# Three of four later modulations summed over rows of w_ada, and queries scaled before they are turned, in a fused trunk layer

## The chip, the core and the metric

The kernel runs on one core of one Trainium2 chip. The metric is the time of one execution on the device in microseconds, the median of several runs. The core's engines are named as the profile names them: PE is TensorE's matmul, PEld its weight load, DVE is VectorE, ACT is ScalarE, POOL is GpSimd, SP is SyncE, which issues nearly all the DMAs.

## What is computed

The program is one layer of a transformer trunk, for 128 context tokens and 512 latent tokens, 1024 wide, all in float32. Two things of it matter here: the modulation, six rows of 1024 for each of the two conditioning vectors, and the attention with its normalised queries.

```python
sh1, sc1, g1, sh2, sc2, g2 = jnp.split(silu(c) @ w_ada + b_ada, 6, axis=-1)   # for c and for c_ctx
u = rms_norm(h, p["g_pre1"]) * (1 + sc1) + sh1
mo, k, v = mixer(u, p, rope_tabs, ctx_k, ctx_v)
h = h + g1 * rms_norm(mo, p["g_post1"])
u = rms_norm(h, p["g_pre2"]) * (1 + sc2) + sh2
h = h + g2 * rms_norm(conv_ffn(u, p), p["g_post2"])
# in mixer:
q, k = rms_norm(q, p["q_norm"]), rms_norm(k, p["k_norm"])      # a head at a time
q_used, keys, vals = rope(q), concat(ctx_k, rope(k)), concat(ctx_v, v)   # latent tokens
att  = softmax(q_used @ keys.T * HEAD_DIM ** -0.5) @ vals @ p["w_att_out"]
conv = (b_gate * dwconv3(c_gate * x_in, p["conv_w"])) @ p["w_conv_out"]
return (sigmoid(g_att) * att + sigmoid(g_conv) * conv) @ p["w_o"], k, v
```

`sh1` and `sc1` are needed at the start. The other four rows, `g1`, `sc2`, `sh2` and `g2`, are needed only after the mixer; these are the later modulations.

## The kernel before

Each product of float32 matrices is made from three products on TensorE: both operands are cut into a high part in a reduced format (fp32r) and the rest (`mm3`, L156). ScalarE copies the high part (`whi`), VectorE subtracts it (`wlo`). Weights come in units of 512 KB into `raw_tile()`, a ring of three buffers; `fetch`, `cut_upto` and `next_unit` load and cut a unit ahead.

The order on TensorE, ScalarE, VectorE and, in the prologue, SP is written out by hand: each engine takes its instructions in the order in which the program states them, and waits where an operand or a buffer is not there yet. The order on SP and POOL is the scheduler's elsewhere.

The stages, with the borders that the profile shows:

- Prologue (to about 75 us): the first modulation, keys and values.
- Attention (75 to 283 us): four groups `g` of four query heads. A group has steps `i` = 0 to 8. `Step(g)` (i = 0) scores the context queries (`scores`, L589), and steps 1 to 8 score one latent tile of 128 queries for two heads each. `most` (L727, L729) takes the row maxima, `exps` (L742) the exponentials with their sums, `shares` (L748, L752) divides on POOL, `turned` (L760, L765) transposes the probabilities, and VectorE or ScalarE copies them out of PSUM as `PT` (L770), `values` (L780, L789) multiplies with the values.
- The queries of tile `t` of group `g`, called (g, t), tile 0 being the context: `q_part` makes them in PSUM, `q_rotate` (`rotate`, L513 to L525) multiplies by the gains and turns the pairs into `qf`; the final sum for latent tiles is L525 on POOL. `squares` and `factors` (L527 to L537) make `rq`, one factor per token and head: ScalarE squares, VectorE sums (L535), POOL scales (L536) and takes the power -0.5 (L537). `q_turn` (L557 to L568, transposes in L560) transposes `qf`, ScalarE and VectorE cut it into `QH` and `QL`. The factor itself is applied behind the scores: `most` multiplies the maxima by `rq`, `exps` has `rq` as its scale.
- In step i, `first` and `then` name the tile that is turned: (g, 2) in step 0, (g, 3) in step 2, (g, 4) and (g+1, 0) in step 5, (g+1, 1) in step 7. The tile (g+1, 2) is made in step 7 of group g and gets its factors in `after2` of step 8; (0, 3) is made ahead of the loop, and `third` gives its rotation and factors in step 1 of group 0, with the turning in step 2.
- Between these, `ada_use` computes the later modulations: 32 units of `w_ada` (1024 rows by 128 columns) in 16 blocks of two. `ada_mm` (L205 to L210) multiplies a unit, as the moving operand, by a 32-column piece of `s32` that holds the two vectors silu(c) and silu(c_ctx) at a place that shifts from unit to unit; each of the four quarters of the array's columns takes two of the eight k-tiles. So 16 units land in different rows of one PSUM tile, and `ada2_keep` adds it to `acc`. `CUTS` and `ring` state in which order units of `w_ada` and of the other weights use the ring of raw buffers. After the loop `ada2_fold` adds the four quarters with `sel`, adds the bias, and multiplies by the gains into `mod`, columns by feature.
- `w_att_out` (283 to 340 us): `plain_gemm`, eight output tiles j of two blocks. While j < 6, twelve pieces of `making` form the combined right-hand sides (`T1` to `T4`) of the next stage. After j = 0 `mod_rows` transposes `mod`, and one DMA writes the 64 rows of the four modulations to `bct` in DRAM.
- The pairs (340 to 574 us): 19 steps m of `mix`, seven block products each, a fast (Strassen) form for the gates and the convolution's inputs. `AH`, `AL` (regions r2 and r3) are free from here, and are taken by `BH`, `BL`.
- `w_conv_out` (574 to 630 us): `plain_gemm` over `BH`, `BL`.
- `w_o`, first half: four quarters q of `us` (630 to 657 us), each quarter all five token tiles, L157 to L159; beside them the weights of the second half are loaded and cut (`half_load`, `half_cut`, L1661 to L1668), and `bload` (L1355 to L1358) spreads the rows `g1` from `bct` over 128 partitions into `WR`. `half_cut(3)` stands in the first quarter. `ZB0`, `ZB1`, `ZB2` (regions r0, r1, r2) hold the right-hand sides of the feed-forward stage.
- Second half of `w_o` with the residual and the second norm (`modulated` is the first to use `sc2` and `sh2`), then the feed-forward network to the end at 1134 us, where `finish` uses `g2`.

The region r0/r1 holds `UH`, `UL` (the normalised input) until the pairs end.

## Time and profile before

| | us |
|---|---|
| median of 3 runs | 1135.46 (1135.44 to 1135.54) |
| span of the profiled execution | 1134.1 |
| PE busy in the attention, 75.0 to 283.5 | 205.04 of 208.50 |
| PE busy in `w_att_out`, the pairs and `w_conv_out`, 283.5 to 629.9 | all 346.4 |
| POOL busy in the attention | 118.89 of 208.50 |
| PE busy behind the first half of `w_o`, 657.5 to 1134.0 | 467.61 of 476.50 |

The page gives the busy time of each engine; the stages are cut out by time windows, whose columns are the busy microseconds and the number of instructions of PE, PEld, DVE, ACT and POOL, the granted TensorE clock, the share of the DMA engines and GB/s. A timeline row has the start and the busy time of an instruction (or of a run of like ones, with "x" their number), engine, line, operation, output and input, shapes, and in brackets how long the engine had stood idle before it, and what released it.

### The profile page before, as it was taken

To read this page: it belongs to the slowest core of one execution; us is meant where nothing else is said; L and a number is where in the kernel's file an instruction comes from. 1 tells how busy PE (TensorE), PEld (TensorE's weight loads), DVE (VectorE), ACT (ScalarE), POOL (GpSimd) and SP (SyncE) were. 2 spreads that over 40 slices of the span, in tenths; PEclk is the share of its full clock that TensorE was granted. 3 is DMA by queue.
4 is the path that set the end of the run, shared out by engine and by line. 5 is a ranking of instruction groups with operands and counts; after the bars stand their busy time and mean duration, and the time that the engine had idled before them with its cause. 6 is when DMAs were issued, how large, how long until landed. Compare 5 with 4: busy or idle time off the path is not lost.

```text
span 1134.1 us, 19512 instructions
## 1 busy us (share of the span) xinstructions
PE 1114.9 (98%) x7885; PEld 1024.5 (90%) x7885; DVE 796.3 (70%) x1269; ACT 569.9 (50%) x979; POOL 158.9 (14%) x198
## 2 busy tenths in 40 slices
PE   7999999999999999999999999999999999999997
PEld 6787888888999999999999889999999999998786
DVE  4587666654656798889645458888788778888544
ACT  4375666665234444545522256655554545555431
POOL 2056566652000000000000012000000000002001
PEclk9999999999999999999999999999999999999999
DMA  9632433333222223223332644233333323315732
GB/s 335 205 92 82 126 94 112 110 96 112 76 75 75 75 77 105 81 75 95 93 111 76 207 164 150 76 99 99 98 112 109 95 91 109 105 61 186 240 99 93
DMA packets 177304, 129.58 MB, mean 114 GB/s; under 512 B 6274, under 2 KB 159422, under 8 KB 177214
## 3 DMA queue, kind: packets, MB, share of 16 engines
q1 hardware_dynamic: 177102, 128.30, 36.4%
q8 instruction: 62, 1.02, 0.4%
q14 instruction: 28, 0.23, 0.1%
q10 hardware_dynamic: 112, 0.04, 0.0%
HBM read 116.87 MB, written 11.45 MB: 113 GB/s over the span
## 4 chain that ended last, share of the span: by engine, by line
PE 89%; DVE 3%; ACT 1%; POOL 0%; issue 0%; DVEq 0%; POOLq 0%; ACTq 0%
PE b L1030 45%; PE b L159 9%; PE b L157 9%; PE b L158 9%; PE s L789 3%; PE s L765 3%; PE s L589 3%; PE s L157 2%; PE s L159 2%; PE s L158 2%; PE s L209 1%; DVE Y L1514 1%; DVE wlo L693 0%; PE s L560 0%; PE b L1421 0%; DVE mx L727 0%
## 5 line engine op out<-in xcount | busy, mean ns | idle before, releaser
L1030 PE MATMUL b<-ZB,whi 128*128 128x322 f32 x1024 | 228.6, 310 | 0.0
L1030 PEld LDWEIGHTS b<-ZB,whi 128*128 128x128 f32 x1024 | 173.8, 189 | 1.6
L1030 PE MATMUL b<-ZB,wlo 128*128 128x322 f32 x512 | 159.4, 311 | 0.0
L1030 PE MATMUL b<-MT,whi 128*128 128x320 f32 x608 | 134.1, 308 | 0.0
L1030 PEld LDWEIGHTS b<-MT,whi 128*128 128x128 f32 x608 | 101.7, 188 | 0.0
L1030 PEld LDWEIGHTS b<-ZB,wlo 128*128 128x128 f32 x512 | 96.2, 188 | 0.0
L1030 PE MATMUL b<-MT,wlo 128*128 128x320 f32 x304 | 93.8, 308 | 0.0
L752 POOL TENSOR_TENSOR pr<-pr,sm 128x640 f32<-128x640 f32 x64 | 80.7, 1270 | 61.1 <-DVE sm L751 61.1
L1017 ACT ACTIVATE whi<-SUM 128x1024 fp32r<-128x1024 f32 x40 | 42.2, 1055 | 79.6 <-DVE SUM L1484 77.2
L1514 DVE SCALAR_TENSOR_TENSOR Y<-C,cffn,Y 128x642 f32<-128x642 f32 x88 | 80.8, 920 | 0.9
L742 ACT ACTIVATE pr<-s,mx,rq 128x640 f32<-128x640 f32 x64 | 56.7, 886 | 38.5 <-DVE mx L729 36.4
L132 DVE TENSOR_TENSOR wlo<-raw,whi 128x1024 fp32r<-128x1024 f32 (+1 forms) x32 | 34.9, 1090 | 52.3 <-ACT whi L131 51.8
L1030 PE MATMUL b<-UH,whi 128*128 128x320 f32 x228 | 70.5, 309 | 0.0
L1030 PE MATMUL b<-UL,whi 128*128 128x320 f32 x228 | 70.4, 309 | 0.0
L1030 PE MATMUL b<-UH,wlo 128*128 128x320 f32 x228 | 70.2, 308 | 0.0
L1021 DVE TENSOR_TENSOR wlo<-raw,whi 128x1024 fp32r<-128x1024 f32 (+1 forms) x51 | 50.4, 1019 | 25.2 <-ACT whi L1017 24.3
L1017 ACT ACTIVATE whi<-WB 128x1024 fp32r<-128x1024 f32 x38 | 40.1, 1056 | 54.8 <-DVE WB L1125 54.8
L157 PE MATMUL s<-whi,UH 128*128 128x256 f32 (+1 forms) x200 | 65.8, 329 | 0.5 <-ACT UH L376 0.4
L727 DVE TENSOR_REDUCE mx<-s 128x1 f32<-128x640 f32 x64 | 52.5, 820 | 17.5 <-PE s L589 17.2
L158 PE MATMUL s<-wlo,UH 128*128 128x256 f32 (+1 forms) x200 | 61.5, 308 | 2.2 <-DVE wlo L693 2.2
L1038 ACT ACTIVATE p<-b 128x322 f32<-128x322 f32 (+1 forms) x78 | 34.3, 439 | 58.2 <-PE b L1030 58.2
L159 PE MATMUL s<-whi,UL 128*128 128x256 f32 (+1 forms) x200 | 61.8, 309 | 0.3
(322 smaller groups left out, 2933.0 us busy)
## 6 DMA issues: line engine op xcount, KB each, us to landing
raw<-in_w_in_dram SPq DMA_DIRECT2D x48, 512.0 KB, 3.6
RAW<-in_w_up_dram SPq DMA_DIRECT2D x40, 512.0 KB, 3.8
raw<-in_w_ada_dram SPq DMA_DIRECT2D x32, 512.0 KB, 4.0
raw<-in_w_down_dram SPq DMA_DIRECT2D x22, 512.0 KB, 4.2
actd<-Y SPq DMA_DIRECT2D x18, 321.0 KB, 2.5
AFB<-actd SPq DMA_DIRECT2D x18, 321.0 KB, 6.8
XT<-in_w_ada_dram SPq DMA_DIRECT2D x9, 512.0 KB, 8.5
raw<-in_w_conv_out_dram SPq DMA_DIRECT2D x9, 512.0 KB, 4.1
```

The source lines that it names most:

```text
L132: eng.tensor_tensor(out=lo[:, :n], in0=raw, in1=hi[:, :n].bitcast(F32), op=ALU.subtract)
L157: PE.matmul(out, ah, bh, start=start, stop=False)
L158: PE.matmul(out, ah, bl, start=False, stop=False)
L159: PE.matmul(out, al, bh, start=False, stop=stop)
L727: V.tensor_reduce(out=mx, in_=self.sc[h], axis=AX.X, op=ALU.max, negate=True)
L742: S.activation(pr, self.sc[h], AF.Exp, bias=mx, scale=rs, accum_out=sm)
L752: G.tensor_tensor(out=pr, in0=pr, in1=sm.broadcast_to((128, NTOK)), op=ALU.mult)
L1017: S.activation(to[0], raw, AF.Copy)
L1021: V.tensor_tensor(out=lo, in0=raw, in1=hi.bitcast(F32), op=ALU.subtract)
L1030: PE.matmul(out, p[:, ws], q[:, k, :], start=start and k == 0 and n == 0, stop=stop and k == 3 and n == 2, skip_group_check=True)
L1038: S.activation(t, pair[j][b], AF.Copy)
L1514: V.scalar_tensor_tensor(out=y, in0=crows(j)[i][:, d:d + NACT], scalar=cffn[:, 44 * d + o:44 * d + o + 1], in1=y, op0=ALU.mult, op1=ALU.add)
```

## The change

It has two parts.

The queries: `q_even` takes the place of `factors` for the tiles made in the loop and for (0, 3). Behind the factors it multiplies `qf` by `rq` on POOL, and notes the tile in the set `even`. For these tiles `most` and `exps` no longer multiply by `rq`; their scale is 1. The turning (`q_turn`, `q_turn_both`) now reads the scaled query. Tiles (0, 0), (0, 1), (0, 2) keep the old way.

The modulations: only `g2` is still made by `ada_use`, in four blocks: one ahead of the loop, and one at step 6 of groups 0 to 2. `ring` is shortened to match. For the other three, the product silu(c) @ w_ada is taken by rows: a DMA loads 128 rows by 1024 columns of `w_ada` (`row_load_ada`), each partition's row is multiplied by its own scalar for the two vectors and added up over the eight row blocks, so that two sums of [128, 1024] are left, and `row_fold` sums over the partitions with a matrix of ones (32 columns) on TensorE, 4 quarters of 256 columns for each vector.

- `g1` during `w_att_out`: `gate_term` at the places `GATE_AT` (VectorE; the first term on ScalarE), rows in `GR`, which has r6b until `T4` takes it at j = 7; the sums lie in `MS`. The pieces of `making` move to `MAKE_AT`. `row_fold`, bias, gain and the DMA to `bct` stand at j = 7 ahead of the preparation for the pairs.
- `sc2` during the pairs m = 0 to 5: `scale_term` multiplies on ScalarE (16 terms, in slots of `mix`); all but the first of each vector go into one of four places of `SP`, from which a DMA issued by POOL with `accum_op=add` adds them to the sum in `SC`. At m = 6 `mod_rows_of` folds, copies and writes the rows to `srow`; `BH`, `BL` take r2, r3 only then.
- `sh2` during `w_conv_out`: `shift_term(j - 1)` at the head of step j on VectorE (first on ScalarE), the rows in `SR` (r1), the sums in `SA` (r0); the last term stands in the first quarter of `w_o`, the fold in front of the second. `room_for` gives r0 and r1 to the feed-forward right-hand sides only behind that.
- `srow` is read back as `srows`, and one transpose with `finished`, behind the first tile of `w_o`'s second half, puts `sc2` and `sh2` into `mod`.

```diff
-        ada_load(ada_raw[i], (2, 4, 3, 5)[i // KT] * D + (i % KT) * 128)
+        ada_load(ada_raw[i], 5 * D + i * 128)
...
         for n in range(2):
-            ada_mm(p, ada_raw[2 * i + n], 2 * ((2 * i + n) % 16), n == 0, n == 1)
+            ada_mm(p, ada_raw[2 * i + n], 2 * (2 * i + n), n == 0, n == 1)
...
     def ada2_keep(i, p, acc):
-        a = acc[:, i // KT * 128:i // KT * 128 + 128]
-        if i % KT == 0:
-            V.tensor_copy(a, p)
+        if i == 0:
+            V.tensor_copy(acc, p)
         else:
-            V.tensor_tensor(out=a, in0=a, in1=p, op=ALU.add)
+            V.tensor_tensor(out=acc, in0=acc, in1=p, op=ALU.add)
+
+    def finished(which, src):
+        b = F_B + (2, 4, 3, 5)[which] * KT
...
     def ada2_fold(acc):
         p = ps1()
-        for i in range(2):
-            PE.matmul(p[:, 32 * i:32 * i + 32], acc[:, i * 128:(i + 1) * 128], sel, start=True, stop=True)
...
+        PE.matmul(p[:, 0:32], acc, sel, start=True, stop=True)
+        finished(3, p[:, 0:16].rearrange("p (f r) -> p r f", r=2))
+
+    def row_term(accs, raw, k):
+        for v in range(2):
+            s = s32[:, 32 * k + 30 + v:32 * k + 31 + v]
+            if k == 0:
+                S.activation(accs[v], raw, AF.Copy, scale=s)
+            else:
+                V.scalar_tensor_tensor(out=accs[v], in0=raw, scalar=s, in1=accs[v], op0=ALU.mult, op1=ALU.add)
+
+    def row_fold(p, accs):
+        for v in range(2):
+            for j in range(4):
+                PE.matmul(p[32 * j:32 * j + 32, 256 * v:256 * v + 256], ones, accs[v][:, 256 * j:256 * j + 256], start=True, stop=True,
+                          tile_position=(0, 32 * j))
+
+    def quarters(x):
+        return x.rearrange("v (j c) -> j v c", c=256)
+
+    def row_load_ada(dst, which, k):
+        nc.sync.dma_start(dst, w_ada[k * 128:(k + 1) * 128, which * D:(which + 1) * D])
...
+        even = set()
+
+        def q_even(sq, g, t):
+            factors(sq, rq[g][:, t, :])
+            G.tensor_tensor(out=qfs[g, t], in0=qfs[g, t], in1=rq[g][:, t, :].unsqueeze(2).broadcast_to((128, 4, HD)), op=ALU.mult)
+            even.add((g, t))
...
-        acc = both[1].rearrange("p a d -> p (a d)")[:, 0:256]
+        acc = both[1].rearrange("p a d -> p (a d)")[:, 0:128]
...
-        ring = ada_raws(0, 1) + [("u", 10), ("u", 11)] + ada_raws(1, 4) + [("u", 12)] + ada_raws(4, 5) + [("u", 13)] + ada_raws(5, 8)
-        ring += [("u", 14)] + ada_raws(8, 9) + [("u", 15)] + ada_raws(9, 12) + [("u", 16)] + ada_raws(12, 15) + [("u", 17)]
-        ring += ada_raws(15, 16) + [("u", 18)]
+        ring = ada_raws(0, 1) + [("u", 10), ("u", 11)] + ada_raws(1, 2) + [("u", 12), ("u", 13)] + ada_raws(2, 3)
+        ring += [("u", 14), ("u", 15)] + ada_raws(3, 4) + [("u", 16), ("u", 17), ("u", 18)]
...
-                    V.tensor_tensor(out=self.mx, in0=self.mx, in1=rq[self.g][:, 0, :], op=ALU.mult)
+                    self.rs = [1.0] * 4
+                    if (self.g, 0) not in even:
+                        V.tensor_tensor(out=self.mx, in0=self.mx, in1=rq[self.g][:, 0, :], op=ALU.mult)
+                        self.rs = [rq[self.g][:, 0, i:i + 1] for i in range(4)]
...
-                rs = rq[self.g][:, 1 + 2 * qh + qi, 2 * pi + h:2 * pi + h + 1]
-                V.tensor_tensor(out=mx, in0=mx, in1=rs, op=ALU.mult)
+                t, rs = 1 + 2 * qh + qi, 1.0
+                if (self.g, t) not in even:
+                    rs = rq[self.g][:, t, 2 * pi + h:2 * pi + h + 1]
+                    V.tensor_tensor(out=mx, in0=mx, in1=rs, op=ALU.mult)
...
-                                     scale=rq[self.g][:, 0, i:i + 1], accum_out=self.sm[:, i:i + 1])
+                                     scale=self.rs[i], accum_out=self.sm[:, i:i + 1])
...
-            after2.append(lambda: factors(sq, rq[0][:, 3, :]))
+            after2.append(lambda: q_even(sq, 0, 3))
...
-                if i in (4, 6, 8) or (i == 1 and g):
+                if i == 6 and g < 3:
                     ada_use(n_ada)()
...
-                        after2.append(lambda: factors(sq, rq[qt[0]][:, qt[1], :]))
+                        after2.append(lambda: q_even(sq, *qt))
...
+    ones = sm_.tile([128, 32], F32, name="ones", bufs=1)
+    G.memset(ones, 1.0)
...
-    for name, tag in (("T1", "r5a"), ("T2", "r5b"), ("T3", "r6a"), ("T4", "r6b")):
+    def turned_sum(name, tag):
         z = rb.tile([128, 2, 4, HT], F32R, tag=tag, name=f"M{name}")
...
+    for name, tag in (("T1", "r5a"), ("T2", "r5b"), ("T3", "r6a")):
+        turned_sum(name, tag)
+    GR = rb.tile([128, 2, D], F32, tag="r6b", name="GR")
+    GACC = [MS[:, v * D:(v + 1) * D] for v in range(2)]
+    row_load_ada(GR[:, 0, :], 2, 0)
+    row_load_ada(GR[:, 1, :], 2, 1)
+
+    def gate_term(k):
+        row_term(GACC, GR[:, k % 2, :], k)
+        if k + 2 < KT:
+            row_load_ada(GR[:, k % 2, :], 2, k + 2)
...
-    Xa, Xb, Xc, Xd = quad(WA, 0), quad(WA, 1), quad(WB, 0), quad(WB, 1)
+    Xa, Xb, Xc, Xd = quad(WA, 0), quad(WA, 1), quad(WB, 0), quad(WA, 0)
...
+    MAKE_AT = (0, 0, 1, 1, 2, 2, 3, 3, 4, 5, 6, 7)
+    GATE_AT = (1, 1, 2, 3, 4, 5, 5, 6)
...
+        if j == 7:
+            turned_sum("T4", "r6b")
+        for i, f in enumerate(making):
+            if MAKE_AT[i] == j:
                 f()
-        elif j == 7:
+        for k in range(KT):
+            if GATE_AT[k] == j:
+                gate_term(k)
+        if j == 5:
+            nc.sync.dma_start(WA[0:128:32, 1280:1536], b_ada[2 * D:3 * D].rearrange("(j c) -> j c", c=256))
+            nc.sync.dma_start(WA[0:128:32, 1536:1792], g_post1[0].rearrange("(j c) -> j c", c=256))
+        if j == 7:
+            pg = bank(3)
+            row_fold(pg, GACC)
+            grow = WA[:, 1792:2304].rearrange("p (v c) -> p v c", v=2)
+            bias, gain = (WA[:, c:c + 256].unsqueeze(1).broadcast_to((128, 2, 256)) for c in (1280, 1536))
+            V.tensor_tensor(out=grow, in0=pg.rearrange("p (v c) -> p v c", v=2), in1=bias, op=ALU.add)
+            V.scalar_tensor_tensor(out=grow, in0=grow, scalar=D ** 0.5, in1=gain, op0=ALU.mult, op1=ALU.mult)
+            nc.sync.dma_start(quarters(bct[0:2 * KT, :].rearrange("(v f) c -> v (f c)", v=2)), grow[0:128:32])
             adds = msums(0)
             adds[0]()
             mhi(0, 0)
@@ -1235,11 +1297,36 @@
...
-            mod_rows(0, 4, sm_, bank(7))
-
...
-    BH = region(ra, "r2", [KT, NTOK], F32R, "BH")
-    BL = region(ra, "r3", [KT, NTOK], F32R, "BL")
+            mod_rows(3, 1, sm_, bank(7))
+
+
+    SC = region(ra, "r2", [5, D], F32, "SC")
+    SP = region(ra, "r3", [5, D], F32, "SP")
+    sums_of, scaled_rows = [SC[:, 0, :], SC[:, 1, :]], [0]
+    row_load_ada(SC[:, 2, :], 4, 0)
+    row_load_ada(SC[:, 3, :], 4, 1)
+    row_load_ada(SC[:, 4, :], 4, 2)
+
+    def scale_term():
+        k, v = divmod(scaled_rows[0], 2)
+        scaled_rows[0] += 1
+        if k >= KT:
+            return
+        room, to = SC[:, 2 + k % 3, :], sums_of[v]
+        if k:
+            to = SP[:, (2 * k + v) % 4, :]
+        S.activation(to, room, AF.Copy, scale=s32[:, 32 * k + 30 + v:32 * k + 31 + v])
+        if k:
+            G.dma_start(out=sums_of[v], in_=to, accum_op=ALU.add)
+        if v and k + 3 < KT:
+            row_load_ada(room, 4, k + 3)
+
+    def mod_rows_of(n, p, accs, to):
+        row_fold(p, accs)
+        S.activation(to, p, AF.Copy)
+        nc.sync.dma_start(quarters(srow[2 * n:2 * n + 2, :]), to[0:128:32, :].rearrange("p (v c) -> p v c", v=2))
+
+    BHL = []
...
+        if m == 6:
+            mod_rows_of(0, bank(5), sums_of, SP[:, 4, 0:512])
+            BHL += [region(ra, f"r{2 + i}", [KT, NTOK], F32R, f"B{x}") for i, x in enumerate("HL")]
+        elif m < 6:
+            for slot in ((0, 3, 4) if m else (1, 3, 4)):
+                also(slot, scale_term)
...
+    SR = region(ra, "r1", [5, D], F32, "SR")
+    SA = region(ra, "r0", [5, D], F32, "SA")
+
+    def shift_term(k):
+        row_term([SA[:, v, :] for v in range(2)], SR[:, k % 5, :], k)
+        if k + 5 < KT:
+            row_load_ada(SR[:, k % 5, :], 3, k + 5)
+
+    for k in range(5):
+        row_load_ada(SR[:, k, :], 3, k)
...
+        if j:
+            shift_term(j - 1)
         _, hi, lo = cut["v", j]
-        outs = plain_gemm(j + 2, hi, lo, BH, BL)
+        outs = plain_gemm(j + 2, hi, lo, *BHL)
...
-    ZB0 = ra.tile([128, 4, 4, HALF], F32R, tag="r0", name="ZB0")
-    ZB1 = ra.tile([128, 4, 4, HALF], F32R, tag="r1", name="ZB1")
-    ZB2 = ra.tile([128, 4, 4, HALF], F32R, tag="r2", name="ZB2")
-    for i, (z, a) in {"B11": (ZB0, 0), "B21": (ZB0, 2), "B22": (ZB1, 0), "T2": (ZB1, 2), "T1": (ZB2, 0), "T3": (ZB2, 2)}.items():
-        TT[i] = (z[:, a], z[:, a + 1])
+    def room_for(tag, one, two):
+        z = ra.tile([128, 4, 4, HALF], F32R, tag=tag, name=f"ZB{tag}")
+        for i, name in enumerate((one, two)):
+            TT[name] = (z[:, 2 * i], z[:, 2 * i + 1])
+
+    room_for("r2", "T1", "T3")
...
+            room_for("r1", "B22", "T2")
...
+        if q == 0:
+            shift_term(KT - 1)
+        elif q == 1:
+            mod_rows_of(1, bank(5), [SA[:, v, :] for v in range(2)], SA[:, 4, 0:512])
+            srows = sm_.tile([64, 128], F32, tag="mrow", name=nm("srows"), bufs=1)[0:32, :]
+            nc.sync.dma_start(srows, srow.rearrange("r (f c) -> (r f) c", c=128))
+            room_for("r0", "B11", "B21")
...
+    pf = bank(7)
+    PE.transpose(pf[:, 0:32], srows, ident[0:32, 0:32])
+    for n in range(2):
+        finished(1 + n, pf[:, 16 * n:16 * n + 16].rearrange("p (r f) -> p r f", r=2))
```

More of the change, by code (lines that the diff above doesn't have):

```diff
@@ L188, in trunk_layer @@
     bct = dp.tile([64, 128], F32, name="bct")
+    srow = dp.tile([4, D], F32, name="srow")
     hd = dp.tile([NT, 128, D], F32, name="hd")
@@ L232, in ada2_fold @@
+    def finished(which, src):
+        b = F_B + (2, 4, 3, 5)[which] * KT
+        V.tensor_tensor(out=mod[:, which], in0=src, in1=feat[:, b:b + KT].unsqueeze(1).broadcast_to((128, 2, KT)), op=ALU.add)
+        if which != 2:
+            gn = (F_POST1, F_PRE2, None, F_POST2)[which]
+            V.tensor_tensor(out=mod[:, which], in0=mod[:, which], in1=feat[:, gn:gn + KT].unsqueeze(1).broadcast_to((128, 2, KT)),
+                            op=ALU.mult)
     def ada2_fold(acc):
         p = ps1()
-        for i in range(2):
-            PE.matmul(p[:, 32 * i:32 * i + 32], acc[:, i * 128:(i + 1) * 128], sel, start=True, stop=True)
@@ L236, in ada2_fold @@
-        for which in range(4):
-            src = p[:, 16 * which:16 * which + 16].rearrange("p (f r) -> p r f", r=2)
-            b = F_B + (2, 4, 3, 5)[which] * KT
-            V.tensor_tensor(out=mod[:, which], in0=src, in1=feat[:, b:b + KT].unsqueeze(1).broadcast_to((128, 2, KT)), op=ALU.add)
-            if which != 2:
-                gn = (F_POST1, F_PRE2, None, F_POST2)[which]
-                V.tensor_tensor(out=mod[:, which], in0=mod[:, which], in1=feat[:, gn:gn + KT].unsqueeze(1).broadcast_to((128, 2, KT)),
-                                op=ALU.mult)
+        PE.matmul(p[:, 0:32], acc, sel, start=True, stop=True)
@@ L966, in trunk_layer @@
                 last = st
-        assert 2 * n_ada == 4 * KT and at_ring[0] == len(ring)
+        assert 2 * n_ada == KT and at_ring[0] == len(ring)
         state["limit"], state["next"] = 1 << 20, 18
```

6 lines of the change are left out of this document (2 added, 4 removed).

## The prediction

> **What bounds the kernel now.** I read the page's busy times first, then the chain that ended last.
>
> ```profile
> span 1134.1 us, 19512 instructions
> PE 1114.9 (98%) x7885; PEld 1024.5 (90%) x7885; DVE 796.3 (70%) x1269; ACT 569.9 (50%) x979; POOL 158.9 (14%) x198
> PE 89%; DVE 3%; ACT 1%; POOL 0%; issue 0%; DVEq 0%; POOLq 0%; ACTq 0%
> ```
>
> TensorE is busy for 98% of the span and makes 89% of the chain. A TensorE instruction taken out is worth its distance in the queue, and a wait put into that queue costs its whole length, unless a later wait shrinks by as much. So I list what leaves the queue, what enters it, and each new wait.
>
> **What leaves.** A block `ada_use` is 16 small products in 32 instructions. One near 172 us, with its neighbours:
>
> ```profile
> 168.18 2.38 PE L789 MATMUL s<-PT,VV 128*64 128x256 f32 x20
> 170.49 1.31 PE L765 MATMUL s<-ident,pr 128*128 128x128 f32 x10
> 171.73 1.08 PE L209 MATMUL s<-raw,s 128*32 128x128 f32 x32
> 172.74 0.33 PE L589 MATMUL s<-KCH,QH 64*128 64x128 f32 x2
> 173.56 0.44 PE L560 MATMUL s<-ident,qf 128*128 128x128 f32 x2
> ```
>
> From the block's start to the next start is 172.74 - 171.73 = 1.01 us. Twelve of sixteen blocks go: -12.1 us.
>
> **What enters.** Three folds (`row_fold`), each 8 products of 256 columns on 32 rows of the array, 16 instructions if they split as the block's do. The nearest row is L789: 20 instructions of 256 columns, on two halves of the array, in 170.49 - 168.18 = 2.31 us, 0.116 each. On four quarters half of that: 16 x 0.058 = 0.92 us a fold, +2.8 us (bounds: the block's 1.01 below, L789's undivided 0.116, so 1.85, above: 2.8 to 5.6, and I stay with the quarters because the blocks run so). One transpose of 32 columns more: +0.2.
>
> **Queries scaled before they are turned.** This is where I expect the gain to be lost. Before, the turning transposes (L560) need only the rotated query; the factors `rq` come later and are used by the softmax. After, POOL multiplies the query by `rq` first, and TensorE waits for it in order, with all that stands behind it. For tile (g+1, 2) the factors are made at the end of step 8 of a group, and the transposes come in step 0 of the next, right behind its 12 score products. The rows of that place:
>
> ```profile
> 172.42 0.41 DVE L535 TENSOR_REDUCE ssq<-sq 128x4 f32<-128x256 f32 x1
> 173.08 1.52 DVE L693 TENSOR_TENSOR wlo<-raw,whi 128x1024 fp32r<-128x1024 f32 x1
> 162.52 0.19 POOL L536 TENSOR_SCALAR ssq<-ssq 128x4 f32<-128x4 f32 x1
> 168.31 0.73 POOL L525 TENSOR_TENSOR qf<-qf,zt 128x256 f32<-128x256 f32 x1 [0.62 <-DVE qf L524]
> 172.27 1.25 POOL L752 TENSOR_TENSOR pr<-pr,sm 128x640 f32<-128x640 f32 x1 [0.34 <-DVE sm L751]
> 173.60 1.05 POOL L536 TENSOR_SCALAR ssq<-ssq 128x4 f32<-128x4 f32 x1
> 174.74 1.02 POOL L537 TENSOR_TENSOR rq<-ssq,mhalf 128x4 f32<-128x4 f32 x1
> ```
>
> POOL finishes the softmax of step 8, then the sum's scaling, then the power: 174.74 + 1.02 = 175.76. The new product has L525's size, 0.73: 176.49. TensorE, with its block gone, is at the transposes at 173.56 - 1.01 = 172.55. It waits 3.9 us, at three transitions (g = 0, 1, 2): +11.8. The POOL times do not come earlier with the shorter queue: they hang on step 8's own transposes, which stand where they stood within the step. L536 took 1.05 instead of 0.19 beside VectorE's subtraction; without that the wait is 3.1, the lower bound 9.2; above, 12.5 if the product meets another such subtraction for 0.2.
>
> [...]
>
> The other tiles have a step between, as (2, 3) here:
>
> ```profile
> 184.34 1.02 POOL L537 TENSOR_TENSOR rq<-ssq,mhalf 128x4 f32<-128x4 f32 x1
> 188.17 0.38 PE L560 MATMUL s<-ident,qf 128*128 128x128 f32 x2
> ```
>
> POOL's power ends at 185.36, the product at 186.1, and the transposes stand at 187.2 with the block gone; so they cost nothing, with about 1 us to spare. But tile (0, 3) has no step between:
>
> ```profile
> 85.93 0.38 PE L560 MATMUL s<-ident,qf 128*128 128x128 f32 x2
> 86.59 3.45 POOL L752 TENSOR_TENSOR pr<-pr,sm 128x640 f32<-128x640 f32 x2
> 87.11 3.47 DVE L693 TENSOR_TENSOR wlo<-raw,whi 128x1024 fp32r<-128x1024 f32 x2
> 88.97 0.39 PE L158 MATMUL s<-wlo,UH 128*128 128x256 f32 x1 [1.09 <-DVE wlo L693]
> 93.10 0.39 PE L158 MATMUL s<-wlo,UH 128*128 128x256 f32 x1 [1.16 <-DVE wlo L693]
> ```
>
> As built, POOL's product stands behind both products L752 of this step: 86.59 + 2 x 1.25 + 0.73 = 89.8, against 85.93, a wait of 3.9. VectorE waits too (its `QL` needs the transposes, the subtractions stand behind it), so the wait at 88.97 stays, but the subtractions no longer collide with POOL, and the wait of 1.16 mostly goes: +2.6 (0 to 4).
>
> **Waits that the blocks covered.** After step 4 of each group, and step 6 of the last, the next scores follow one block sooner. They need the PSUM tile that VectorE still empties:
>
> ```profile
> 198.80 0.82 DVE L770 COPY PT<-s 128x640 f32<-128x640 f32 x1 [0.84 <-PE s L765]
> 199.24 1.08 PE L209 MATMUL s<-raw,s 128*32 128x128 f32 x32
> ```
>
> The copy ends at 199.62, the scores could start at 199.24: 0.38 us, five times, +1.9 (0 to 2). The products `mx` by `rq` that fall away on VectorE lie beside TensorE's work and are worth nothing here, nor are the adds of `acc`.
>
> **The three stages that sum rows.**
>
> ```profile
> 283.50:340.20 56.70, 56.70 (x389) 56.66 (x388) 32.23 (x30) 19.10 (x26) 0.00 (x0) 1.00 0.26 75
> 340.20:573.60 233.40, 233.40 (x1594) 233.40 (x1593) 182.74 (x266) 114.58 (x178) 0.00 (x0) 1.00 0.29 83
> 573.60:629.90 56.30, 56.30 (x386) 56.30 (x385) 28.00 (x37) 14.45 (x18) 0.18 (x3) 1.00 0.32 96
> 665.39 1.28 DVE L1404 SCALAR_TENSOR_TENSOR WR<-TX,root,WR 128x1024 f32<-128x1024 f32 x1 [0.31 <-POOL root L1396]
> 666.59 0.68 DVE L1388 TENSOR_TENSOR TX<-b,WR 128x512 f32<-128x512 f32 x1
> 642.64 1.06 ACT L1017 ACTIVATE whi<-raw 128x1024 fp32r<-128x1024 f32 x1 [7.60 <-DMA raw<-in_w_o_dram]
> ```
>
> Columns are PE, PEld, DVE, ACT, POOL, clock, DMA, GB/s. A term of a row costs VectorE 666.59 - 665.39 = 1.20 us (same form and size), ScalarE 1.06. First stage: 14 x 1.20 = 16.8 on VectorE's 32.2 of 56.7: it fits. Placed by j, VectorE is through with the last term at about 332.4, and TensorE's fold (one eighth before the stage's end) is due at 332.4: +0.3 (0 to 2). The loads `GR` go on SP one step ahead, and the weights behind them two steps ahead: nothing. Second: 16 terms on ScalarE in six pairs of 233.4/19 = 12.3 us, 17 of 74 us, where half is free. The first term waits for its row, issued when `AH` is last read; ScalarE then has 5 us behind it and needs them: +0.3 (0 to 2). Third: 28.0 + 16.8 of 56.3: fits.
>
> The third fold does not. It stands ahead of the second quarter of `w_o`, and the last shift term stands behind the subtraction of the weights for `half_cut(3)` on VectorE. SP, as built, now issues that load behind the two of `bct` into `WR`, which wait for the last product of the stage before:
>
> ```profile
> 627.39 0.37 SPq L1663 DMA_DIRECT2D raw<-in_w_o_dram  x1
> 629.91 0.82 SPq L1357 DMA_DIRECT2D WR<-bct  x2
> 634.32 1.22 DVE L1021 TENSOR_TENSOR ZB<-raw,ZB 128x1024 fp32r<-128x1024 f32 x1
> 636.76 0.39 PE L157 MATMUL b<-whi,MHa 128*128 128x512 f32 x1
> 629.90:636.70 6.80, 6.80 (x31) 5.58 (x31) 5.64 (x6) 3.58 (x4) 0.17 (x3) 1.00 0.90 306
> L139 SPq DMA_DIRECT2D raw<-in_w_o_dram x4: 368/368/395, 606.3 to 634.4; - x4
> DMA to landing us min/median/max: 6.3/6.3/6.3
> ```
>
> So the load goes out at 630.7 instead of 627.4, behind 1 MB more, at 306 GB/s in all: 1.5 MB take 5 us, and it lands at 635.7 (a neighbour took 6.3). ScalarE 1.06, subtraction 1.22, two terms 2.4, half a fold 0.5: 640.9, where 636.6 + 0.9 = 637.5 was due: +3.4. Bounds: 0, if SP's order costs nothing; 5.4 with a landing of 7.
>
> **The accumulating DMAs.** Fourteen, seven in a chain for each row, issued on POOL, which is idle there. No row shows one. Below, a plain load; above, three passes, 10.8:
>
> ```profile
> raw<-in_w_in_dram SPq DMA_DIRECT2D x48, 512.0 KB, 3.6
> ```
>
> The first goes out some 9 us into the pairs, the fold stands at 6 x 12.3 = 73.9: each may take 65/7 = 9.3 us before anything waits, ScalarE's ring of four rooms included. I take about 6, with no wait. [...]
>
> **Sum.** -12.1 + 2.8 + 0.2 + 11.8 + 2.6 + 1.9 + 0.3 + 0.3 + 3.4 = +11.2, so a span of 1145.3. The runs' median, 1135.46, lies 1.4 above the profiled span; I keep that: 1146.7 us. Adding the lower bounds gives -12.1 + 2.8 + 0.2 + 9.2 = +0.1, the upper -12.1 + 5.6 + 0.2 + 12.5 + 4 + 2 + 2 + 2 + 5.4 = +21.6; they won't all fall on one side, so this case's own range is 1139 to 1153.
>
> **Rivals.**
> - *The TensorE sum alone* (11%): no new wait. For it speaks that TensorE is the bound; against it that POOL would have to end each product at 172.6, not 176.5: it decides only if the chain ahead of the product is 3.9 us shorter. -12.1 + 3.0 = -9.1: 1126.4 us.
> - *The transitions alone* (9%): only the three waits at their lower bound cost, the rest finds cover in TensorE's queue: +0.1, 1135.6 us. The 1 us to spare elsewhere speaks for it; SP's order against it.
> - *The accumulations are the bound* (14%): at 10.8 us each the chain of seven ends at 9 + 75.6 = 84.6, 10.7 us past its fold, so ScalarE and then TensorE stand: 1157.4 us. It decides from 9.3 us on. A plain load's 3.6 speaks against it.
> - *The change does not do what it says*: as built, 192 of the small products are gone and 14 accumulations there, so no chance is kept for this.
>
> **Numbers.** The forecast has 66%, 1146.7. The range, 1136 to 1155, holds nearly all of it and what lies toward the two middle rivals. About 0.2%, 2.3 us, is what a measurement can tell from no change. Faster: the first rival and a part of the second, 0.13. Same: the rest of the second, 0.07. Slower: 0.80.
>
> **What would show it.** Right: TensorE's waits in front of the turning transposes, released by POOL, of near 4 us three times in step 0 and one near 85 us; blocks L209 down to four; a wait of some 3 us in front of the third fold, released by VectorE; POOL's DMAs under 9.3 us each. Wrong: transposes that start within 1 us of the scores' end; no wait at the third fold; a fold at the seventh pair that waits for a DMA.

## The result and the profile after

The changed kernel takes 1160.18 us (median of 4 runs, 1158.49 to 1164.11) beside 1135.45 (1134.21 to 1135.54): ratio 1.0226, 95% interval 1.0207 to 1.0245. The direction was forecast; of the 24.7 us, 11.2 were. The profiled execution has a span of 1157.8 us, 23.7 more than before. From its page and from the view of TensorE's waits (who waited for whom, microseconds in total, times, longest):

```profile
span 1157.8 us, 18950 instructions
PE 1119.2 (97%) x7548; PEld 1025.6 (89%) x7548; DVE 819.1 (71%) x1226; ACT 583.6 (50%) x1001; POOL 179.9 (16%) x230
```

```profile
PE s L587 <- POOL qf L581: 15.2, 4, 3.9
PE b L256 <- DVE SA L251: 4.1, 1, 4.1
PE b L1063 <- DVE WB L1074: 2.7, 1, 2.7
PE b L157 <- ACT ACTa L1635: 2.0, 1, 2.0
```

The three upper waits are new. L587 is the turning, L256 the fold, L1063 a block product of the pairs; the fourth is as in the kernel before. TensorE has 337 instructions less, and yet more busy time, 1119.2 us instead of 1114.9. That is the first sign of what the prediction left out: the instructions that remain got slower.

Where the time goes, by stage, worked out from the starts of the first product of each stage in the two timelines (attention: from the first context scores of group 0; the last border but one is the first product with the weights that `half_cut(3)` makes):

| stage | before | after | forecast difference | measured |
|---|---|---|---|---|
| attention | 209.88 | 219.42 | +4.2 | +9.5 |
| `w_att_out` | 56.43 | 57.63 | +1.2 | +1.2 |
| pairs | 234.07 | 240.31 | +1.2 | +6.2 |
| `w_conv_out` | 56.32 | 56.31 | 0 | 0 |
| `w_o` to the weights of `half_cut(3)` | 30.83 | 38.74 | +4.3 | +7.9 |
| rest | 473.40 | 472.38 | +0.2 | -1.0 |

The transition from group 1 to group 2, on POOL and on TensorE, as the prediction worked it out from the same place before:

```profile
177.31 1.25 POOL L783 TENSOR_TENSOR pr<-pr,sm 128x640 f32<-128x640 f32 x1 [0.65 <-DVE sm L782]
178.64 1.05 POOL L556 TENSOR_SCALAR ssq<-ssq 128x4 f32<-128x4 f32 x1
179.78 1.02 POOL L557 TENSOR_TENSOR rq<-ssq,mhalf 128x4 f32<-128x4 f32 x1
180.87 0.61 POOL L581 TENSOR_TENSOR qf<-qf,rq 128x256 f32<-128x256 f32 x1
```

```profile
176.77 0.33 PE L616 MATMUL s<-KCH,QH 64*128 64x128 f32 x2
...
181.54 0.67 PE L587 MATMUL s<-ident,qf 128*128 128x128 f32 x2 [3.88 <-POOL qf L581]
```

The chain on POOL is the forecast one (1.05 and 1.02 again, the product 0.61 instead of 0.73), and the wait of 3.88 us the forecast 3.9. What comes next was not forecast. Windows of TensorE at that place; columns are the window, its length, PE busy and its number, the granted clock, the DMA share, GB/s:

```profile
172.00:177.60 5.60, 5.60 (x56) 1.00 0.01 1
177.60:181.60 4.00, 0.12 (x3) 1.00 0.15 38
181.60:185.00 3.40, 3.40 (x17) 0.50 0.36 109
185.00:190.00 5.00, 5.00 (x47) 1.00 0.01 3
```

After the wait TensorE is granted half its clock for 3.4 us; the two transposes of L587 take 0.67 us where they took 0.44. In windows of 0.1 us, all such stretches between the first scores and the end of the FFN:

| behind the wait at | wait, us | half clock from - to | length | busy time lost |
|---|---|---|---|---|
| tile (0, 3) | 3.57 | 89.4 - 92.9 | 3.41 | 1.7 |
| (1, 2) | 3.88 | 127.0 - 133.8 | 6.83 | 2.7 |
| (2, 2) | 3.88 | 181.6 - 185.0 | 3.41 | 1.7 |
| (3, 2) | 3.88 | 232.8 - 239.6 | 6.83 | 2.9 |
| pairs | 2.69 | 389.8 - 393.2 | 3.41 | 1.7 |
| third fold | 4.13 | 656.1 - 662.9 | 6.83 | 2.5 |

Lost is taken as half of the time in which TensorE was busy at half clock, 13.2 us in all, an estimate: behind the third fold, products of 512 columns started 0.43 us apart at half clock (661.10 to 662.80) and 0.23 us apart after it. The kernel before has one stretch in these stages, 1052.7 to 1056.1 in the feed-forward network (1.7 us); the changed one has none there, and its rest is 1.0 us shorter.

In all six of the table the granted clock is 0.50; three last 3.41 us and three 6.83 us.

The wait in the pairs has another cause. SP's load, VectorE and TensorE there:

```profile
375.77 0.38 SPq L1155 DMA_DIRECT2D raw<-in_w_in_dram  x1
```

```profile
386.55 0.69 DVE L1170 TENSOR_TENSOR WB<-raw 128x512 f32<-128x512 f32 x1 [4.05 <-DMA raw<-in_w_in_dram]
```

```profile
388.39 0.53 PE L1063 MATMUL b<-MT,whi 128*128 128x320 f32 x2 [2.69 <-DVE WB L1074]
```

A load of weights that went out at 375.77 landed at 386.5, 10.7 us later, where the median was 3.9 in this stage before. The next two fences have the stage's windows (PE, PEld, DVE, ACT, POOL, clock, DMA share, GB/s), before and after; the last line is from the view of the DMAs (median to landing):

```profile
350.00:410.00 60.00, 60.00 (x411) 60.00 (x410) 46.55 (x67) 30.67 (x48) 0.00 (x0) 1.00 0.31 88
```

```profile
360.00:420.00 60.00, 57.31 (x379) 56.84 (x378) 42.32 (x58) 39.95 (x56) 12.09 (x14) 0.97 0.99 227
```

```profile
SC<-SP POOLq DMA_DIRECT2D x14, 512.0 KB, 6.4
```

An accumulating DMA takes 6.4 us, close to the 6 assumed, and the fold of this row never waits for it. But the DMA engines, 31% busy here before, are at 99%.

The third fold waits along the chain that the prediction worked out. SP, ScalarE, VectorE, TensorE:

```profile
646.73 0.81 SPq L1463 DMA_DIRECT2D WR<-bct  x2
647.64 0.38 SPq L1769 DMA_DIRECT2D raw<-in_w_o_dram  x1
```

```profile
654.30 1.06 ACT L1050 ACTIVATE ZBr<-raw 128x1024 fp32r<-128x1024 f32 x1 [4.35 <-DMA raw<-in_w_o_dram]
```

```profile
656.54 2.47 DVE L251 SCALAR_TENSOR_TENSOR SA<-SR,s,SA 128x1024 f32<-128x1024 f32 x2
```

```profile
657.87 2.28 PE L256 MATMUL b<-SA,ones 128*32 128x256 f32 x16 [4.13 <-DVE SA L251]
```

The load stands behind the two of `bct`, lands 6.7 us after its issue, and the last shift term comes behind its subtraction. The fold itself takes 2.28 us here, where one at full clock took 1.07: its second half waits for the second vector's term, at half clock.

### The profile page after: what moved, and what is told of

Read it like the earlier page. It is cut to its first block, busy times and chain, and to the rows that moved or that the text cites. A ratio compares the mean times of both kernels' runs of the same rounds, so it can differ in the third digit from the quotient of the medians.

```text
span 1157.8 us, 18950 instructions
## 1 busy us (share of the span) xinstructions
PE 1119.2 (97%) x7548; PEld 1025.6 (89%) x7548; DVE 819.1 (71%) x1226; ACT 583.6 (50%) x1001; POOL 179.9 (16%) x230
## 4 chain that ended last, share of the span: by engine, by line
PE 89%; DVE 4%; DMA 3%; POOL 1%; ACT 1%; issue 1%; SPq 0%; DVEq 0%; POOLq 0%; ACTq 0%
PE b L1063 43%; PE b L157 9%; PE b L159 9%; PE b L158 9%; PE s L820 3%; PE s L616 3%; PE s L796 3%; PE s L157 3%; PE s L159 3%; PE s L158 2%; DVE Y L1620 1%; DMA raw<-in_w_in_dram 1%; DMA XT<-in_w_ada_dram 1%; DMA WR<-in_x_sample_dram 1%; PE s L587 1%
## 5 line engine op out<-in xcount | busy, mean ns | idle before, releaser
L1063 PE MATMUL b<-ZBr,whi 128*128 128x322 f32 x1008 | 225.0, 310 | 0.0
L1063 PEld LDWEIGHTS b<-ZBr,whi 128*128 128x128 f32 x1008 | 171.1, 189 | 1.6
L1063 PE MATMUL b<-ZBr,wlo 128*128 128x322 f32 x504 | 156.9, 311 | 0.0
L1063 PE MATMUL b<-MT,whi 128*128 128x320 f32 x608 | 134.7, 309 | 2.7 <-DVE WB L1074 2.7
L1063 PEld LDWEIGHTS b<-MT,whi 128*128 128x128 f32 x608 | 101.8, 188 | 2.9 <-issue 2.9
L1063 PEld LDWEIGHTS b<-ZBr,wlo 128*128 128x128 f32 x504 | 94.7, 188 | 0.0
L1063 PE MATMUL b<-MT,wlo 128*128 128x320 f32 x304 | 94.4, 310 | 0.0
L1063 PE MATMUL b<-UH,whi 128*128 128x320 f32 x228 | 71.1, 312 | 0.0
L1063 PE MATMUL b<-UL,whi 128*128 128x320 f32 x228 | 70.9, 311 | 0.0
L1063 PE MATMUL b<-UH,wlo 128*128 128x320 f32 x228 | 70.6, 310 | 0.0
L157 PE MATMUL s<-whi,UH 128*128 128x256 f32 (+1 forms) x200 | 68.2, 341 | 0.7 <-ACT UH L396 0.5
L756 DVE TENSOR_REDUCE mx<-s 128x1 f32<-128x640 f32 x64 | 50.0, 819 | 17.0 <-PE s L616 16.7
L1063 PEld LDWEIGHTS b<-MT,wlo 128*128 128x128 f32 x304 | 57.2, 188 | 0.6 <-DVE wlo L1054 0.5
```

The source lines that it names most:

```text
L157: PE.matmul(out, ah, bh, start=start, stop=False)
L756: V.tensor_reduce(out=mx, in_=self.sc[h], axis=AX.X, op=ALU.max, negate=True)
L1063: PE.matmul(out, p[:, ws], q[:, k, :], start=start and k == 0 and n == 0, stop=stop and k == 3 and n == 2, skip_group_check=True)
```

## The experiments

Stage times of the profiled executions, in us, from the same starts as above:

| kernel | time | attention | `w_att_out` | pairs | `w_o` to `half_cut(3)` | rest |
|---|---|---|---|---|---|---|
| before | 1135.45 | 209.88 | 56.43 | 234.07 | 30.83 | 473.40 |
| after | 1160.18 | 219.42 | 57.63 | 240.31 | 38.74 | 472.38 |
| a1, old scaling | 1145.07 | 203.80 | 57.63 | 240.96 | 38.77 | 472.36 |
| a2, queries alone | 1150.07 | 222.57 | 56.43 | 234.07 | 30.83 | 473.32 |
| a3, 27 transposes | 1157.52 | 212.58 | 57.62 | 243.22 | 38.62 | 472.37 |
| a4, additions on POOL | 1176.71 | 219.49 | 57.63 | 255.97 | 39.45 | 472.12 |
| a5, late fold | 1151.37 | 217.84 | 57.63 | 238.23 | 31.84 | 473.55 |
| a8, early factors | 1139.92 | 199.58 | 57.62 | 240.87 | 38.93 | 472.67 |
| a9, half the accumulations | 1157.83 | 218.42 | 57.63 | 237.41 | 38.43 | 472.37 |
| a10, mixed | 1130.22 | 201.89 | 57.63 | 234.28 | 31.84 | 473.32 |
| b3, before with early factors | 1133.46 | 208.29 | 56.44 | 234.07 | 30.83 | 471.82 |
| b4, a10 with the old scaling | 1134.66 | 206.11 | 57.63 | 234.07 | 31.84 | 473.81 |

Times are medians of all runs. Kernels with many waits scatter by some microseconds, and the mean granted clock with them: the changed one took 1158.49 us at 0.985 and 1164.11 us at 0.981.

### a1: the queries' part undone

```diff
             factors(sq, rq[g][:, t, :])
-            G.tensor_tensor(out=qfs[g, t], in0=qfs[g, t], in1=rq[g][:, t, :].unsqueeze(2).broadcast_to((128, 4, HD)), op=ALU.mult)
-            even.add((g, t))
```

> The changed kernel with the queries' part undone: the factors are applied behind the scores again, all three row sums stay. Theory: TensorE's four waits in front of the turning transposes (15.2 us in the changed kernel's profile) go, and with them the stretches of half clock behind them, 3.4, 5.5, 3.2 and 5.9 us of busy time at 0.50, so 9.0 us: 1160.2 - 24.2 = 1136. Rival: the half clock comes from the thinner queue in the attention, where twelve blocks are gone, and not from the waits; then only the waits go: 1145.

1145.07 us, between the two. The waits at the turning are gone and the attention stays at full clock, so the half clock came with the waits and not with the thinner queue. But the attention is only 6.1 us shorter than before, where twelve blocks are worth 12.1. From its view of TensorE's waits in the attention:

```profile
PE s L158 <- DVE wlo L717: 2.2, 2, 1.2
...
PE s L614 <- ACT pr L765: 1.4, 3, 0.5
...
PE s L614 <- ACT PT L799: 0.7, 4, 0.2
```

The scores wait for exponentials, and the two waits for the weights `wlo`, which the changed kernel no longer had, are back. So the rival had the sum right by another way: the blocks covered waits. Of the 6.0 us that are missing, the changed kernel loses 2.2 as well (a copy out of PSUM, see the account of the prediction); most of the rest is something that the queries' part does away with (a8, b3, b4).

### a2: the queries' part alone, in the kernel before

```diff
-            after2.append(lambda: factors(sq, rq[0][:, 3, :]))
+            after2.append(lambda: q_even(sq, 0, 3))
...
-                        after2.append(lambda: factors(sq, rq[qt[0]][:, qt[1], :]))
+                        after2.append(lambda: q_even(sq, *qt))
```

with `q_even`, `most` and `exps` as in the change.

> The kernel before with the queries' part alone: all sixteen blocks stay, the product by the factors stands ahead of the turning. Theory: the waits are one block shorter than in the changed kernel, 2.9 us at the three transitions, and about 3.6 at tile (0, 3), which had no block ahead of it; together 12.3, so 1147.8 if the clock holds, and up to 1155 if each wait is followed by a stretch at half clock as in the changed kernel; the waits of 2.9 us tell whether shorter ones drop the clock too. Rival: the wait only takes the place of VectorE's wait for the weights, and POOL catches up: within 3 us of before.

1150.07 us. The view of waits and the three transitions of TensorE's timeline:

```profile
PE s L567 <- POOL qf L561: 12.2, 4, 3.6
```

```profile
128.76 0.44 PE L567 MATMUL s<-ident,qf 128*128 128x128 f32 x2 [2.88 <-POOL qf L561]
...
181.09 0.44 PE L567 MATMUL s<-ident,qf 128*128 128x128 f32 x2 [2.88 <-POOL qf L561]
...
234.99 0.44 PE L567 MATMUL s<-ident,qf 128*128 128x128 f32 x2 [2.87 <-POOL qf L561]
```

The waits have the lengths worked out. The clock fell behind (0, 3), (2, 2) and (3, 2), for 3.41 us each, and not behind (1, 2): equal waits, unequal results. The attention is 12.7 us longer; waits and half clock make 12.2 + 5.1 = 17.3, less the 2.2 of the waits for `wlo`, so some 2.4 us came back in other steps. Seen from here, taking out the twelve blocks brings the changed kernel 3.15 us in the attention, while its waits are 3.0 and its half clock 3.9 us longer: 10.1 us of the 12.1.

### a3, b1, b2: work in place of standing still

```diff
             p = ps1() if p is None else p
+            if (g and t == 2) or (g, t) == (0, 3):
+                for _ in range(27):
+                    PE.transpose(p[:, 0:128], ident, ident)
```

and the same with 9 and 18.

> The changed kernel with 27 transposes of the identity put in front of the turning of (1, 2), (2, 2), (3, 2) and (0, 3), into the PSUM tile that the turning then overwrites: TensorE works for about 3.4 us where it stood still, and nothing starts earlier. Theory: the half clock follows from standing still; the granted clock stays at 1.00 behind the four places, and the time falls by the 9 us that the half clock cost, to 1151. Rival: the half clock comes from something else (the products with 320 columns that follow, or the row sums): no change, 1160, and the clock falls at the same places.

1157.52 us. The third place, in windows of PE:

```profile
177.20:181.00 3.80, 3.02 (x28) 1.00 0.17 48
181.00:184.40 3.40, 3.40 (x29) 1.00 0.35 105
```

The turning starts as late behind the scores as in the changed kernel, 0.78 us of the wait is left, and the clock holds at all four places. The attention falls by 6.8 us: the 9.0 less what the fill costs (four times 3.17 us of transposes and 3.0 of waits are 15.7 us, not 15.2, and a wait for `wlo` of 0.8 is back). So it was standing still that halved the clock at these four places. Of the whole time only 2.7 us is left of this: in this profile the first scores started 2.2 us later, behind a stretch at half clock from 19 to 26 us, and the wait in the pairs was 3.6 us, with another of 1.5; there and behind the third fold the clock fell all the same.

> The changed kernel with 9 transposes of the identity instead of 27 at the four places, so that TensorE still stands for about 2.8 us at each. One look, at the granted clock behind the four places. [...] Rival: a fixed length decides; then it is all four or none.

> The same with 18 transposes, TensorE stands for about 1.8 us at each place. Theory: the clock is halved at one place at most. Rival (any wait of a few microseconds halves it): at three or four.

1161.58 and 1157.9 us, one run each. With 2.60 to 2.75 us left the clock fell at three places of four, with 1.61 to 1.77 us at one. Counted at these places, and at the fourth wait of the first view, over all profiles of this study:

| TensorE stood for | where | clock fell |
|---|---|---|
| 3.57 to 3.88 us | the turning in after, a2's (0, 3), a4, a5, a9 | 17 of 17 |
| 2.60 to 2.88 | a2's transitions, b1 | 5 of 7 |
| 1.98 to 2.00 | the fourth wait, all fourteen profiles | 5 of 14 |
| 1.61 to 1.77 | b2 | 1 of 4 |
| 0.63 to 0.78 | a3 | 0 of 4 |

The one case of b2 had a second wait, of 0.67 us, in front of the fall. No fixed length parts the cases: the clock held behind a2's wait of 2.88 us in front of (1, 2) and b1's of 2.75 us there, and fell behind five of the waits of 1.98 to 2.00 us (before, a2, a5, a10, b4). What parts equal waits was not shown.

### a4 and a9: the accumulations

a4 puts them on POOL as instructions, a9 makes the second vector's on VectorE:

```diff
-            G.dma_start(out=sums_of[v], in_=to, accum_op=ALU.add)
+            G.tensor_tensor(out=sums_of[v], in0=sums_of[v], in1=to, op=ALU.add)
```

```diff
+        if k and v:
+            V.scalar_tensor_tensor(out=to, in0=room, scalar=s32[:, 32 * k + 30 + v:32 * k + 31 + v], in1=to, op0=ALU.mult, op1=ALU.add)
+            if k + 3 < KT:
+                row_load_ada(room, 4, k + 3)
+            return
```

> The changed kernel with the fourteen accumulating DMAs replaced by fourteen additions of 128 by 1024 on POOL. Theory: the accumulations fill the 16 DMA queues (share 0.98 to 1.08 in the pairs) and so make a load of weights land in 10.7 us where 3.9 is the rule; without them the share falls to about a half, the wait of 2.7 us in the pairs and the half clock behind it (3.4 us, so 1.7) go: 1160.2 - 4.4 = 1155.8. Rival: the load is late because SP issues it behind the loads of the rows, whatever the accumulations do; then the wait stays and the time is 1160, or more where POOL's additions and VectorE hold each other up.

> The changed kernel with the second vector's seven accumulations of sc2 made on VectorE (one instruction of 128 by 1024 each, 1.2 us) and only the first vector's seven by accumulating DMAs. Theory: the share of the DMA queues falls from about 1.0 to 0.8 between 360 and 420 us, no load of weights takes over 7 us, the wait of 2.7 us and the half clock behind it go, and VectorE's 8.4 us more find room: the pairs take 236 us instead of 240.3, 1155.8. Rival: it is not the number of accumulations but SP's order, or VectorE is full: the pairs stay at 240 or more.

a4 took 1176.71 us, worse than either theory: its pairs take 256 us. The loads are on time (median 3.7 us, no wait for a DMA on VectorE), which is what the theory said of them. But the additions on POOL take some 2.5 us each (from 360 to 420 us POOL is busy for 27.96 us with 11 instructions), and VectorE's sums of the weights stand beside it. By form, busy and mean ns, in a4:

```profile
L1170 DVE TENSOR_TENSOR WB<-raw 128x512 f32<-128x512 f32 x5 | 10.1, 2015 | 0.0
L1170 DVE TENSOR_TENSOR WB<-raw,raw 128x512 f32<-128x512 f32 x5 | 9.9, 1974 | 0.0
```

In the changed kernel these take 687 and 686 ns. So this run can't weigh the accumulations by its time.

a9 does weigh them. Windows of the stage:

```profile
360.00:420.00 60.00, 59.11 (x398) 58.16 (x396) 53.23 (x71) 35.97 (x54) 5.19 (x6) 1.00 0.77 185
```

The DMA share is 0.77, the wait for the late load and the half clock are gone, and the pairs take 237.4 us (236 expected, 240.3 in the changed kernel). The loads of the rows are the same eight in a9, so the number of accumulations decides. Its time, 1157.83, was 2 us above the expectation.

### a5: the third fold one quarter later

```diff
-        elif q == 1:
+        elif q == 2:
             mod_rows_of(1, bank(5), [SA[:, v, :] for v in range(2)], SA[:, 4, 0:512])
```

> The changed kernel with the third fold one quarter of w_o later (ahead of the third instead of the second). Theory: the fold waited 4.1 us for VectorE's last term and the half clock behind it cost some 2.5 us more; one quarter is 6.8 us, so the term is there and both go, 1160.2 - 6.5 = 1153.7, and the stretch from the start of w_o to the feed-forward network falls from 38.7 to about 32.2 us (30.8 in the kernel before, and 1.0 for the fold). Rival: the way over DRAM to the transpose behind the first tile of the second half gets too short, and TensorE waits there for the DMA instead: 1157 or more.

1151.37 us. The stretch takes 31.84 us: the kernel before's 30.83 and the fold's 1.01. No wait comes in its place.

### a8: factors early in step 8

```diff
                 for h in range(1 if st.ctx else 2):
                     st.most(h)
+                    if i == 8 and h == 0:
+                        for f in after2:
+                            f()
+                        after2 = []
                     st.exps(h)
...
             factors(sq, rq[g][:, t, :])
+            if (g, t) == (0, 3):
+                return
```

> The changed kernel with the factors and the product for tile (g+1, 2) made between the two row maxima of step 8 instead of at its end, and tile (0, 3) scaled behind the scores as before. Theory: POOL's chain ends about 3 us earlier, the three waits of 3.9 us shrink to about 0.3 each, the clock stays at 1.00, and VectorE's two waits of 2.2 us in all come back at (0, 3): 1160.2 - 15.2 - 9.0 + 0.9 + 2.2 = 1139; from the first scores to w_att_out 198 us. Rival: the blocks' cover is what is missing, as in the kernel with the queries' part undone, whose attention took 203.8 us: 1145.

1139.92 us. POOL and TensorE at the transition to group 2:

```profile
166.66 0.19 POOL L556 TENSOR_SCALAR ssq<-ssq 128x4 f32<-128x4 f32 x1 [0.49 <-DVE ssq L555]
166.93 1.02 POOL L557 TENSOR_TENSOR rq<-ssq,mhalf 128x4 f32<-128x4 f32 x1
167.92 1.25 POOL L785 TENSOR_TENSOR pr<-pr,sm 128x640 f32<-128x640 f32 x1
169.14 0.61 POOL L583 TENSOR_TENSOR qf<-qf,rq 128x256 f32<-128x256 f32 x1
```

```profile
169.80 0.44 PE L589 MATMUL s<-ident,qf 128*128 128x128 f32 x2
```

The product ends at 169.75, the turning starts at 169.80 without a wait, and the clock holds. The attention takes 199.6 us, 10.3 us less than before, against 6.1 in a1, with the same twelve blocks gone. a8 differs from a1 in two things: the query is scaled ahead of the scores, and the factors of tile (g+1, 2) are made earlier in step 8. No run parts the two; where the 4.2 us between them lie is said in the account of the prediction.

### a10, b3, b4: a version that beats both, and which part brings it

a10 joins a8 and a5, and makes `sc2` in blocks again:

```diff
-        ada_load(ada_raw[i], 5 * D + i * 128)
+        ada_load(ada_raw[i], (4, 5)[i // KT] * D + (i % KT) * 128)
...
-                if i == 6 and g < 3:
+                if i == 4 or (i == 6 and g < 3):
                     ada_use(n_ada)()
```

with `ring` and the finishing of `sc2` to match, and without `SC`, `SP` and `scale_term`. b3 is the kernel before with a8's queries, b4 is a10 with the old scaling and with the factors back at the end of step 8.

> Early factors and the late fold as above, and sc2 back in blocks on TensorE (eight blocks instead of four, no accumulations, no fold in the pairs); g1 and sh2 stay sums over rows. Theory: eight blocks of 1.01 us go, two folds of 1.1 come, the transitions wait 0.3 us each, the pairs are those of the kernel before: span 73.1 + 202.7 + 57.6 + 234.1 + 56.3 + 32.1 + 473 = 1129, time 1130, faster than both. Rival: as in the kernel with the queries' part undone, about half of what the blocks free is lost to the softmax that they covered: 1134, no change that can be told.

> The kernel before with the queries' part alone in its early form (factors between the two maxima of step 8, tile (0, 3) as before); all sixteen blocks stay. Theory: the shorter softmax (no multiplication between maximum and exponential) gives TensorE little while the blocks cover it, about 0.5 us a group: 1133.5. Rival: the queries' part is itself the gain of the mixed version: 1131 or less.

> The mixed version with the queries' part undone: eight blocks are gone, the factors stand behind the scores. Theory: without the shorter softmax the steps that lost their block wait for the exponentials, as in the kernel with the queries' part undone, where twelve blocks brought 6.1 us in the attention instead of 12: the attention takes about 205.5 us instead of 201.9, 1133.9. Rival: eight blocks leave cover enough: 1130.

a10: 1130.22 us (1130.20 to 1130.24, 4 runs), ratio to before 0.9954 (0.9939 to 0.9969). b3: 1133.46, ratio 0.9988 (0.9976 to 0.9999). b4: 1134.66, ratio 0.9998 (0.9989 to 1.0007). So neither part alone brings what the two bring together: without a8's queries, eight blocks fewer and two sums over rows in their place make no difference that can be told.

## Why the prediction was wrong

- *The step that failed* is the rule of the first part, that a wait in TensorE's queue "costs its whole length, unless a later wait shrinks by as much". Here six waits, of 2.69 to 4.13 us, cost more: the granted clock fell to 0.50 at each. 13.2 us of half clock were priced nowhere, while the kernel before's trace had a case to read, the 1.7 us lost at 1052.7 to 1056.1 behind a wait of 1.98 us. In a3 the same lateness without standing still keeps the clock at 1.00. This alone takes the time out of the range's upper end.
- *The transitions* were right in place, releaser and length: 3.88 us against 3.9, three times. a8 shows that the place of the factors in step 8 decides: moved ahead, nothing waits.
- *Tile (0, 3)*: the wait was 3.57 us (3.9 forecast) and took the place of 2.2 us of VectorE's waits, so 1.4 net of the clock instead of 2.6.
- *"The products `mx` by `rq` that fall away on VectorE ... are worth nothing here"*: wrong. While all blocks are there, a8's queries make the attention 1.6 us shorter (b3 against before). With twelve blocks gone, a1's attention is 4.2 us longer than a8's. Of these the view of TensorE's waits shows 1.8. By the starts of the steps, 1.1 us lie in step 0 of groups 1 to 3, 1.2 in step 1, 0.7 in step 2, 0.8 in step 4, and 0.4 in step 7 of the last group. In steps 0 and 1 the earlier factors may have a part; steps 2, 4 and 7 speak for the scaling.
- *Waits that the blocks covered*: right, 1.9 us forecast and 2.2 measured. By the starts of the steps, step 5 of each group and step 7 of the last take 0.43 us longer in the changed kernel than before, at the five places forecast. The view of waits does not show it: the first score product starts at 155.01, the second only at 155.45, when VectorE's copy has ended at 155.39, and TensorE counts as busy in between. In group 1, the changed kernel (VectorE, TensorE), then the same scores before:

```profile
154.57 0.82 DVE L801 COPY PT<-s 128x640 f32<-128x640 f32 x1 [1.01 <-PE s L796]
```

```profile
155.01 0.85 PE L616 MATMUL s<-KH,QH 64*128 64x320 f32 x2
```

```profile
156.02 0.41 PE L589 MATMUL s<-KH,QH 64*128 64x320 f32 x2
```

- *The accumulating DMAs*: the latency was right (6.4 us, about 6 forecast) and so was the chain, which never makes the fold wait. The step looked at their chain alone. With them the DMA engines are 99% busy from 360 to 420 us, and a load of weights that took 10.7 us made TensorE wait 2.69 us and lose 1.7 us of clock. The rival of the accumulations, 1157.4 us, came near the time by another mechanism: not the seventh accumulation decides, but the load beside them.
- *The third fold*: the chain from SP's order to the last term was right. The load went out at 647.6 and landed 6.7 us later (5 forecast, up to 7 in the bounds), the wait was 4.1 us (3.4 forecast), with 2.5 us of half clock behind it. a5 takes both away.
- *Blocks and folds*: a fold takes 1.01 us of the queue, 0.92 forecast. In the steps where nothing else changes (step 8 of groups 0 to 2), a block taken out is worth the 1.01 us forecast.

The sum with these sizes: 11.2 forecast, +13.2 for the clock, +2.7 for the wait in the pairs, +0.7 at the fold, +0.2 for two folds' size, -1.7 for the stretch at half clock that the rest no longer has, -1.6 for the shorter softmax, +0.3 for the cover, -1.2 at (0, 3): 23.8, where 23.7 us lie between the profiles. That it comes so close is in part luck: by stage it misses by up to 1.2 us (10.7 in the attention, where 9.5 were measured), and the misses cancel.

## What to carry to other kernels

Where TensorE is the bound, price a wait of 3.6 us or more as its length and the 1.7 to 2.9 us of half clock that such waits cost here, a shorter one by the counts of the table (5 of 7 at 2.60 to 2.88 us, 5 of 14 at 2 us, none of 4 under 0.8 us), and look for the stretches at half clock that the kernel before already has. A step that turns from "applied later" to "needed first" is paid at the tightest place of the loop: list each place with its slack, and move the chain ahead there before giving the step up. Work given to DMA queues was not free here while its own chain was on time (the engines' share went from 0.31 to 0.99, and one load took 10.7 us where the median had been 3.9): add its share to what the engines carry in that stage, and ask which other load lands late.

## What was not expected of the hardware

- The six stretches at half clock in the changed kernel were 3.41 or 6.83 us long. Waits of 2.0 us were followed by one in 5 cases of 14, a2's waits of 2.9 us at two places of three. The changed kernel's four runs, 1158.49 to 1164.11 us, had mean granted clocks of 0.985, 0.985, 0.981 and 0.982, the slowest with the lowest.
- Fourteen accumulating DMAs of 512 KB took 43.9% of the 16 DMA engines over 90 us, the 10.8 MB of plain traffic beside them 39.4%: 2.8 us of all the engines for an accumulation, 1.7 for 512 KB of plain loads.
- With a4's additions of 128 by 1024 on POOL, ten of VectorE's sums of 512 columns took 2.0 us (mean 2015 and 1974 ns) instead of 0.69.
